# Squares of the SSD outputs get two tiles of their own instead of the tiles shared with the tanh of the silus

## The chip, the cores and the metric

The kernel runs on one core of one Trainium2 chip. The metric is the device time of one execution in microseconds (us). The kernel before takes 1710.79 us, the median of three runs (1707.15 to 1713.31).

## The reference

One layer of a hybrid recurrent decoder. A prompt of 2048 tokens and 8 samples of 8 tokens each (2112 rows of 1024 channels) are normalised and multiplied with one wide matrix (`w_in`). Three branches work on the product: a Mamba-2 style SSD scan, an RG-LRU and an S5. Their outputs, 2048 channels, are multiplied with `w_out`, added to the input and normalised again. Of the SSD branch this matters:

```
xbc = silu(causal_conv(xbc))                # 16 channel blocks of 128: x (8), B (4), C (4)
y   = ssd_scan(x, dt, a, B, C) + d * x      # chunks of 128 tokens, a state handed from chunk to chunk
y   = y * silu(z)
y_ssd = rmsnorm(y) * ssd_norm_g             # the mean of y*y over all 1024 SSD channels of a token
```

The mean needs the squares of all SSD outputs, summed over the channel blocks. The kernel adds them up, block by block, in tiles `sqacc`.

## The kernel before, in words

Channels lie on the 128 partitions, tokens on the free axis. The tokens are cut in five segments (`SEGS`): s = 0 to 3 are 512 prompt tokens each, s = 4 the 64 sample tokens. The input projection of one channel block and one segment is `in_proj` (L235): 24 matmuls of 512 columns, L247 to L249, into one bank of PSUM out of a ring of three (`pmm`). float32 is carried in two float16 halves, hence three matmuls per step.

The phases follow one another: projections and S5 inputs, S5, RG-LRU with the GLU, then the SSD branch, which fills about 697 to 1362 us of the profile, and last the output projection (L1175 to L1177). In the SSD branch `ssd_group` (L624) is called for four groups g = 0 to 3. For each segment (the sample segment goes with s = 2) it does three things.

- `channels` (L631), four times: two blocks of x, one of B, one of C. `in_proj`; ScalarE copies the bank to `raw` (L340, three buffers); the convolution is one ScalarE instruction (L353) and three on VectorE (L355); then silu: ScalarE writes a tanh into a tile `th` (L641) and VectorE forms `(th + 1) * x` (L642).
- `ssd_chunk` (L556), four times: transposes (L545, L546), scores (L520), the decay `e` (L524, L525 on ScalarE, L531 on VectorE), outputs into `ps_y` (L568, L571), the state (L573, L577, L578), and the outputs back into the x tiles (L582).
- `gated` (L645), twice, for the two x blocks: a gate `pz`, the product `x * pz` (L655 on VectorE), its store and its square `sq` on ScalarE (`Row.add`, L380 to L387; the square is L384), and on GpSimd the addition `sqacc += sq` (L662). For groups 0 and 1 `pz` was computed earlier and is loaded by a DMA (L650). For groups 2 and 3 it is computed here by `gate` (L357): an `in_proj`, a tanh into a tile `th` (L362 on ScalarE) and `pz = (th + 1) * ps` on VectorE (L363), which also sets the PSUM bank free.

The pool `st` has two buffers per tag. In the kernel before the tag `th` serves the tanh of `channels`, the tanh of `gate` and the squares `sq`; the tag `pz` is separate and has two buffers as well. For the first x block of group 0 the square goes straight into `sqacc`.

The order of each engine's queue is not written out by hand. A planner goes through the program with a simulated time line and places on each engine the earliest instruction of the program that is ready in its simulation, so that work of later segments can be drawn forward where an engine would idle. A tile that has no free buffer holds its writer back in that plan, too. The engines then run their queues in the planned order. Pools of different phases share memory (`sx` on the left side takes the place of the GLU's pool), and a tile waits for those tiles before it that lay at its addresses.

Of the kernel before, what the change touches and what calls it, by code (L numbers as in the profile page):

```python
# [8 lines left out]
F32 = mybir.dt.float32  # L9
# [15 lines left out]
SG = 512  # L25
SEGS = [(0, SG), (SG, SG), (2 * SG, SG), (3 * SG, SG), (SEQ, NS)]
# [16 lines left out]
def hymba_step_kernel(  # L43
# [11 lines left out]
    st = ctx.enter_context(tc.tile_pool(name="st", bufs=2))  # L55
# [28 lines left out]
    def col(nm, i, src=cols):  # L84
        c = COL[nm] + i
        return src[:, c:c + 1]
# [141 lines left out]
    def w_ahead(n=1):  # L228

        for c0 in W_ORDER[len(WB):len(WB) + n]:  # L230
            WB[c0] = Block(c0)
# [3 lines left out]
    def in_proj(w, s):  # L235

        n = SEGS[s][1]
        blocks = list(WB.values())
        for i, b in enumerate(blocks):
            if b.done is None and blocks[i - 6].left:  # L240
                b.age += 1
                if b.age > AGE:
                    b.finish()
            b.left = b.left or (b.w is w and s == 3)
        ps = bank(pmm, "mm", "ps_mm")
        for k in range(KD):
            P.matmul(ps[:, :n], lhsT=w[:, 0, k, :], rhs=XH[s][:, k, :], start=(k == 0), stop=False)  # L247
            P.matmul(ps[:, :n], lhsT=w[:, 0, k, :], rhs=XL[s][:, k, :], start=False, stop=False)  # L248
            P.matmul(ps[:, :n], lhsT=w[:, 1, k, :], rhs=XH[s][:, k, :], start=False, stop=(k == KD - 1))  # L249
        return ps[:, :n]  # L250

    def seg_tile(tag, name, s, pool, w=SG, bufs=None, wsmp=NS):
        if s == 4:
            return pool.tile([128, wsmp], F32, name=name + "s", tag=tag + "s", bufs=2 if pool is st else 1)
        return pool.tile([128, w], F32, name=name, tag=tag, bufs=bufs)
# [71 lines left out]
    def conv_raw(ps, un, s, tl, stT):  # L327

        raw = seg_tile("raw", "raw", s, st, SG + 3, 3, 88)
        if s == 4:  # L330
            rv = raw.rearrange("p (b e) -> p b e", e=11)
            G.tensor_copy(rv[:, :, 0:3], stT.rearrange("p (b e) -> p b e", e=3))
            A.activation(out=rv[:, :, 3:11], in_=ps.rearrange("p (b e) -> p b e", e=8), func=AF.Copy, scale=un)
            G.tensor_copy(tl.t27[:, 1:9, :], rv[:, :, 8:11])
            return raw
        if s == 0:
            G.memset(raw[:, 0:3], 0.0)
        else:
            G.tensor_copy(raw[:, 0:3], tl.halo)
        A.activation(out=raw[:, 3:SG + 3], in_=ps, func=AF.Copy, scale=un)  # L340
        tl.halo = tl.t27[:, 0, :] if s == 3 else tmp.tile([128, 3], F32, name="halo", tag="halo", bufs=6)
        G.tensor_copy(tl.halo, raw[:, SG:SG + 3])
        return raw

    def conv(out, raw, s, w, b):
        if s == 4:
            o = out.rearrange("p (b e) -> p b e", e=8)
            rv = raw.rearrange("p (b e) -> p b e", e=11)
            tap = [rv[:, :, j:j + 8] for j in range(4)]
        else:  # L350
            o = out
            tap = [raw[:, j:j + SG] for j in range(4)]
        A.activation(out=o, in_=tap[0], func=AF.Identity, scale=w[0], bias=b)  # L353
        for j in range(1, 4):
            V.scalar_tensor_tensor(o, tap[j], w[j], o, op0=ALU.mult, op1=ALU.add)  # L355

    def gate(ps, un2, s):  # L357

        n = SEGS[s][1]
        th = seg_tile("th", "th", s, st)  # L360
        pz = seg_tile("pz", "pz", s, st)
        A.activation(out=th, in_=ps, func=AF.Tanh, scale=un2)  # L362
        V.scalar_tensor_tensor(pz, th, 1.0, ps, op0=ALU.add, op1=ALU.mult)  # L363
        return pz
# [191 lines left out]
    def ssd_chunk(sp, g, xs, BT, CT, c, H):  # L556
        q0 = (c * 128) % SG
        bcq = sp.tile([128, 4, 128], F32, name="bcq", tag="bcq")
        S.dma_start(out=bcq, in_=aT[c, 4 * g:4 * g + 4, :].unsqueeze(0).to_broadcast([128, 4, 128]))
        xdt, xw, bs = transposed(sp, xs, BT, q0, 128, g, c)  # L560
        m = scores(sp, g, BT, CT, q0, 128, bcq, c)
        yp = bank(pss, "y", "ps_y")
        if c:
            ce = c_decayed(sp, CT, q0, 128, eT[c, 4 * g:4 * g + 4, :])
        o = [yp[64 * (h % 2):64 * (h % 2) + 64, (h // 2) * 128:(h // 2) * 128 + 128] for h in range(4)]
        for j in range(2):
            for h in (2 * j, 2 * j + 1):
                P.matmul(o[h], lhsT=xdt[:, h, :], rhs=m[:, h, :], start=True, stop=(c == 0))  # L568
            if c:
                for h in (2 * j, 2 * j + 1):  # L570
                    P.matmul(o[h], lhsT=H[:, h, :], rhs=ce[:, h, :], start=False, stop=True)  # L571
        ps = bank(pss, "s", "ps_s")
        P.matmul(ps[:, 0:256], lhsT=bs, rhs=xw.rearrange("p h e -> p (h e)"), start=True, stop=True)  # L573
        hn = sp.tile([128, 4, 64], F32, name="hst", tag="hst")
        spv = ps[:, 0:256].rearrange("p (h e) -> p h e", h=4)
        if c:
            G.tensor_tensor(hn, H, dec[:, c, 4 * g:4 * g + 4].unsqueeze(2).to_broadcast([128, 4, 64]), op=ALU.mult)  # L577
            V.tensor_tensor(hn, hn, spv, op=ALU.add)  # L578
        else:
            V.tensor_copy(hn, spv)  # L580
        for j in range(2):
            V.scalar_tensor_tensor(xs[j][:, q0:q0 + 128], xs[j][:, q0:q0 + 128], dpair[:, 2 * g + j:2 * g + j + 1],  # L582
                                   yp[:, j * 128:(j + 1) * 128], op0=ALU.mult, op1=ALU.add)
        return hn
# [39 lines left out]
    def ssd_group(sx, sp, g, done):  # L624
        blks = [2 * g, 2 * g + 1, 8 + g, 12 + g]
        ws = [WB[c0] for c0 in SB(g)]
        rows = [Row(k, unz[:, k:k + 1] if k < ZE else WB[k]) for k in (2 * g, 2 * g + 1)]
        tls = [Tail(b) for b in blks]
        H = None

        def channels(i, s):  # L631

            w, un, _ = ws[i]
            b = blks[i]
            raw = conv_raw(in_proj(w, s), un, s, tls[i], stS[:, b, :])
            if s == 3:
                w_ahead()
            x = seg_tile("xxbc"[i] + str(i % 2), "x", s, sx if i < 2 else sp, SG, 5 if i < 2 else 2)
            conv(x, raw, s, [col("sconv_w", 16 * j + b, hcols) for j in range(4)], col("sconv_b", b, hcols))
            th = seg_tile("th", "th", s, st)  # L640
            A.activation(out=th, in_=x, func=AF.Tanh)  # L641
            V.scalar_tensor_tensor(x, th, 1.0, x, op0=ALU.add, op1=ALU.mult)  # L642
            return x

        def gated(j, s, y):  # L645
            k = 2 * g + j
            s0, n = SEGS[s]
            if k < ZE:
                pz = seg_tile("pz", "pz", s, st)
                S.dma_start(out=pz, in_=zb[k, :, s0:s0 + n])  # L650
            else:
                pz = gate(in_proj(WB[k][0], s), WB[k][2], s)
                if s == 3:
                    w_ahead()
            V.tensor_tensor(y, y, pz, op=ALU.mult)  # L655
            if g == 0 and j == 0:
                sqacc[s] = sx.tile([128, SEGS[s][1]], F32, name="sqacc", tag=f"sqacc{s}", bufs=1)
                rows[j].add(s, y, sqacc[s])
            else:
                sq = seg_tile("th", "sq", s, st)  # L660
                rows[j].add(s, y, sq)
                G.tensor_tensor(sqacc[s], sqacc[s], sq, op=ALU.add)  # L662

        for segs in SSD_ORD:
            xb = {s: [] for s in segs}
            for i in range(4):
                for s in segs:
                    xb[s].append(channels(i, s))
            for s in segs:
                x0, x1, BT, CT = xb[s]  # L670
                if s == 4:
                    ssd_sample(sp, g, (x0, x1), BT, CT)
                else:
                    for c in range(4 * s, 4 * s + 4):
                        H = ssd_chunk(sp, g, (x0, x1), BT, CT, c, H)
            if 3 in segs:
                S.dma_start(out=o_ssd_p[g], in_=H)
                done()
            for j in range(2):
                for s in segs:  # L680
                    gated(j, s, xb[s][j])
# [608 lines left out]
    sx = pool(sA, "ssx", "left")  # L1290
# [8 lines left out]
    for i, (t0, n) in enumerate(TT_):  # L1299
        s = min(t0 // SG, 4)  # L1300
# [143 lines left out]
```

## Time and profile before

| | |
|---|---|
| time, median of three | 1710.79 us |
| the profiled execution's own time | 1712.97 us |
| its span in the profile | 1711.3 us |
| TensorE (PE) busy | 1594.9 us, 93% |
| VectorE (DVE) busy | 1108.0 us, 65% |
| ScalarE (ACT) busy | 861.3 us, 50% |
| GpSimd (POOL) busy | 534.0 us, 31% |

The profile is of one execution. A page gives busy times per engine and the groups of instructions that cost most; further views give busy times in chosen stretches, the instructions of one engine in order of time, who waited for whom, and the chain of work that ended last. A number in brackets behind an instruction is the time its engine sat idle ahead of it, with the instruction that ended this. PEclk is the clock that TensorE was granted, as a share of full speed.

### The profile page before, as it was taken

The numbers are of one execution on the slowest core, as the hardware profiler recorded it, in microseconds if no ns is written. First come the engines' busy times: TensorE is split into PE (matmuls) and PEld (weight loads), VectorE is DVE, ScalarE is ACT, GpSimd is POOL, SyncE is SP. The second block draws the span as 40 slices with busy tenths as digits, with TensorE's granted clock in tenths as the row PEclk, the third lists the DMA queues.
The fourth block names the chain that finished last, engine by engine and source line by source line (L and its number), as shares of the span: only waits on it lengthen the run. The fifth ranks groups of instructions, "written<-read, shape, count | busy, mean of one in ns | idle before, by whom it ended". The sixth has DMA issues, their size and how long they took to land.

```text
span 1711.3 us, 26615 instructions
## 1 busy us (share of the span) xinstructions
PE 1594.9 (93%) x9474; PEld 823.3 (48%) x9474; DVE 1108.0 (65%) x2643; ACT 861.3 (50%) x1913; POOL 534.0 (31%) x822
## 2 busy tenths in 40 slices
PE   6899898898899999999999968999999699999998
PEld 3554544454444444455555544555555444444443
DVE  7844578996676575678778566677777734633332
ACT  7723424443787776657466455566765421422210
POOL 1213226764131111344545555544454200000000
PEclk9999899999989999999999989999999699999999
DMA  7412322232325242333324253243325521633100
GB/s 241 127 46 53 113 93 89 90 101 68 99 85 156 80 138 66 105 86 122 117 91 131 86 153 81 69 142 115 115 93 191 175 80 63 207 99 99 43 25 31
DMA packets 143941, 178.17 MB, mean 104 GB/s; under 512 B 66424, under 2 KB 92480, under 8 KB 143808
## 3 DMA queue, kind: packets, MB, share of 16 engines
q1 hardware_dynamic: 143808, 176.47, 33.9%
q8 instruction: 74, 1.21, 0.3%
q14 instruction: 59, 0.48, 0.1%
HBM read 126.57 MB, written 48.69 MB: 102 GB/s over the span
## 4 chain that ended last, share of the span: by engine, by line
PE 47%; DVE 5%; ACT 4%; DMA 2%; issue 2%; POOL 2%; SPq 0%; POOLq 0%; ACTq 0%; DVEq 0%
PE ps_o L1175 7%; PE ps_o L1177 7%; PE ps_o L1176 6%; PE ps_mm L247 6%; PE ps_mm L248 6%; PE ps_mm L249 6%; PE ps_y L568 2%; DVE x L355 2%; PE ps_s L573 2%; PE ps_y L571 1%; DMA ce<-eT 1%; PE ps_g L520 1%; PE ps_tp L545 1%; DMA w<-in_w_blk_dram 1%; PE ps_o L1205 1%
## 5 line engine op out<-in xcount | busy, mean ns | idle before, releaser
L247 PE MATMUL ps_mm<-xh,whl 128*128 128x512 f16 x1280 | 494.0, 386 | 18.1 <-DVE pz L363 12.8
L248 PE MATMUL ps_mm<-xl,whl 128*128 128x512 f16 x1280 | 493.5, 386 | 0.0
L249 PE MATMUL ps_mm<-xh,whl 128*128 128x512 f16 x1280 | 492.6, 385 | 0.9 <-DVE whl L206 0.9
L248 PEld LDWEIGHTS <-whl 128*128 128x128 f16 x1600 | 155.9, 99 | 168.5 <-issue 38.3
L247 PEld LDWEIGHTS <-whl 128*128 128x128 f16 x1600 | 159.6, 101 | 149.1 <-issue 17.8
L249 PEld LDWEIGHTS <-whl 128*128 128x128 f16 x1600 | 156.4, 99 | 153.5 <-issue 18.1
L1175 PE MATMUL ps_o<-wo,yt 128*128 128x512 f16 x512 | 195.6, 382 | 10.2 <-ACT yt L1186 5.2
L1176 PE MATMUL ps_o<-wo,yt 128*128 128x512 f16 x512 | 195.6, 382 | 0.0
L1177 PE MATMUL ps_o<-wo,yt 128*128 128x512 f16 x512 | 194.7, 381 | 0.0
L355 DVE SCALAR_TENSOR_TENSOR x<-raw,hcols,x 128x512 f32<-128x512 f32 x192 | 158.5, 830 | 23.3 <-ACT x L353 20.6
L524 ACT ACTIVATE e<-bcq,acum 128x128 f32<-128x128 f32 (+1 forms) x272 | 86.1, 386 | 58.9 <-PE ps_y L568 52.5
L1186 ACT ACTIVATE yt<-y,rsc 128x256 f16<-128x256 f32 (+1 forms) x144 | 56.7, 477 | 106.0 <-PE ps_o L1177 81.0
L538 POOL TENSOR_TENSOR ce<-ce,x 128x512 f32<-128x512 f32 x60 | 84.8, 1422 | 66.8 <-DMA ce<-eT 31.8
L1347 ACT ACTIVATE yo<-res 128x1024 f32<-128x1024 f32 x16 | 16.8, 1050 | 153.4 <-DVE res L1195 153.4
L1195 DVE SCALAR_TENSOR_TENSOR res<-ps_o,rsu,res 128x512 f32<-128x512 f32 x32 | 24.0, 750 | 94.9 <-PE ps_o L1177 94.9
L1175 PEld LDWEIGHTS <-yt 128*128 128x128 f16 x512 | 50.5, 99 | 66.3 <-ACT yt L1186 5.6
L1176 PEld LDWEIGHTS <-yt 128*128 128x128 f16 x512 | 50.4, 98 | 66.3 <-issue 6.9
L363 DVE SCALAR_TENSOR_TENSOR pz<-th,ps_mm 128x512 f32<-128x512 f32 x64 | 43.6, 682 | 57.8 <-ACT th L362 57.3
L531 DVE TENSOR_TENSOR e<-e,gm 128x512 f32<-128x512 f32 (+1 forms) x68 | 57.2, 842 | 36.8 <-POOL gm L530 32.9
L1177 PEld LDWEIGHTS <-yt 128*128 128x128 f16 x512 | 50.3, 98 | 61.3 <-issue 0.8
L340 ACT ACTIVATE raw<-ps_mm,sc_out 128x512 f32<-128x512 f32 x80 | 54.2, 677 | 39.8 <-PE ps_mm L249 37.6
L362 ACT ACTIVATE th<-ps_mm,sc_out 128x512 f32<-128x512 f32 x64 | 43.6, 681 | 52.1 <-PE ps_mm L249 51.5
(450 smaller groups left out, 3012.8 us busy)
## 6 DMA issues: line engine op xcount, KB each, us to landing
w<-in_w_blk_dram SPq DMA_DIRECT2D x40, 512.0 KB
bcq<-aT SPq DMA_DIRECT2D x64, 256.0 KB
y<-ysp SPq DMA_DIRECT2D x16, 1024.0 KB
ce<-eT SPq DMA_DIRECT2D x60, 256.0 KB
xt<-in_x_dram SPq DMA_DIRECT2D x16, 512.0 KB
ysp<-x SPq DMA_DIRECT2D x32, 256.0 KB
wo<-in_w_out_dram SPq DMA_DIRECT2D x16, 512.0 KB
res<-in_x_dram SPq DMA_DIRECT2D x16, 512.0 KB
```

Source lines behind the costliest of these rows:

```text
L247: P.matmul(ps[:, :n], lhsT=w[:, 0, k, :], rhs=XH[s][:, k, :], start=(k == 0), stop=False)
L248: P.matmul(ps[:, :n], lhsT=w[:, 0, k, :], rhs=XL[s][:, k, :], start=False, stop=False)
L249: P.matmul(ps[:, :n], lhsT=w[:, 1, k, :], rhs=XH[s][:, k, :], start=False, stop=(k == KD - 1))
L340: A.activation(out=raw[:, 3:SG + 3], in_=ps, func=AF.Copy, scale=un)
L355: V.scalar_tensor_tensor(o, tap[j], w[j], o, op0=ALU.mult, op1=ALU.add)
L524: A.activation(out=e[:n, h, :n], in_=bcq[:n, h, :n], func=AF.Relu, scale=-1.0, bias=acum[:n, c, 4 * g + h:4 * g + h + 1])
L531: V.tensor_tensor(e[:n, :, :n], e[:n, :, :n], gm.unsqueeze(1).to_broadcast([n, 4, n]), op=ALU.mult)
L538: G.tensor_tensor(ce[:, :, :n], ce[:, :, :n], CT[:, q0:q0 + n].unsqueeze(1).to_broadcast([128, 4, n]), op=ALU.mult)
L1175: P.matmul(ps, lhsT=h, rhs=w[:, 0, c], start=(k == 0), stop=False)
L1176: P.matmul(ps, lhsT=h, rhs=w[:, 1, c], start=False, stop=False)
L1177: P.matmul(ps, lhsT=l, rhs=w[:, 0, c], start=False, stop=(k == nk - 1))
L1186: A.activation(out=hl[:, k, 0, :n], in_=r[:, k, :n], func=AF.Copy, scale=c)
```

## The change

The square of an SSD output no longer takes a tile of the tag `th`. It gets a tag `sq` of its own with two buffers of 128 x 512 float32 in the pool `sx` (4 KB more per partition). For the sample segment a part of the wide tile is used, where before there was a narrow one (`ths`). No instruction is added or taken away.

```
-                sq = seg_tile("th", "sq", s, st)
+                sq = sx.tile([128, SG], F32, name="sq", tag="sq", bufs=2)[:, :SEGS[s][1]]
                 rows[j].add(s, y, sq)
                 G.tensor_tensor(sqacc[s], sqacc[s], sq, op=ALU.add)
```

## Rows read from the trace of the kernel before

**Rows 1.** Busy time in stretches: us; busy (instructions) per engine; PEclk; DMA share; GB/s
```profile
697.00:985.00 288.00, 284.70 (x1922) 156.92 (x1919) 212.81 (x407) 168.82 (x395) 139.91 (x220) 1.00 0.37 108
985.00:1054.00 69.00, 49.36 (x325) 28.58 (x324) 41.47 (x87) 35.72 (x93) 36.18 (x47) 0.83 0.46 124
1054.00:1330.00 276.00, 268.33 (x1915) 149.74 (x1910) 204.89 (x435) 169.65 (x393) 131.06 (x187) 0.99 0.38 119
1330.00:1362.00 32.00, 19.09 (x83) 12.39 (x82) 24.21 (x55) 16.41 (x35) 7.63 (x8) 0.57 0.41 134
1362.00:1711.30 349.30, 339.37 (x1628) 155.24 (x1626) 141.61 (x331) 75.39 (x183) 2.87 (x3) 0.99 0.26 86
```
**Rows 2.** TensorE in order of time: start, us, instruction, [idle before <- releaser]
```profile
987.30 0.44 PE L545 MATMUL ps_tp<-id,x 128*128 128x128 f32 x2 [2.14 <-DVE x L642]
996.24 0.38 PE L249 MATMUL ps_mm<-xh,whl 128*128 128x512 f16 x1
1021.86 1.53 PE L545 MATMUL ps_tp<-id,x 128*128 128x128 f32 x4 [7.48 <-DVE x L642]
1036.45 0.44 PE L568 MATMUL ps_y<-e,xdt 128*64 128x128 f32 x4 [0.89 <-DVE e L531]
1040.08 0.44 PE L571 MATMUL ps_y<-ce,hst 128*64 128x128 f32 x4 [1.30 <-POOL ce L538]
1044.78 0.58 PE L247 MATMUL ps_mm<-xh,whl 128*128 128x512 f16 x1 [3.82 <-DVE pz L363]
1254.61 0.38 PE L247 MATMUL ps_mm<-xh,whl 128*128 128x512 f16 x1 [0.71 <-ACT raw L340]
1355.61 0.59 PE L1175 MATMUL ps_o<-wo,yt 128*128 128x512 f16 x1 [2.71 <-DVE y_m L115]
```
**Rows 3.** ScalarE in order of time, squares and tanhs
```profile
1018.46 0.71 ACT L384 ACTIVATE sq<-x,unz 128x512 f32<-128x512 f32 x1
1019.93 0.63 ACT L641 ACTIVATE th<-x 128x512 f32<-128x512 f32 x1 [0.67 <-POOL sqacc L662]
1023.27 0.69 ACT L362 ACTIVATE th<-ps_mm,sc_out 128x512 f32<-128x512 f32 x1
1042.63 0.71 ACT L384 ACTIVATE sq<-x,sc_out 128x512 f32<-128x512 f32 x1
1043.34 0.66 ACT L362 ACTIVATE th<-ps_mm,sc_out 128x512 f32<-128x512 f32 x1
```
**Rows 4.** VectorE in order of time: products, gates and the silu's second step
```profile
1015.55 0.69 DVE L655 TENSOR_TENSOR x<-x,pz 128x512 f32<-128x512 f32 x1
1016.48 0.69 DVE L655 TENSOR_TENSOR x<-x,pz 128x512 f32<-128x512 f32 x1
1024.61 0.68 DVE L363 SCALAR_TENSOR_TENSOR pz<-th,ps_mm 128x512 f32<-128x512 f32 x1
1174.36 1.69 DVE L642 SCALAR_TENSOR_TENSOR x<-th,x 128x512 f32<-128x512 f32 x1
1354.88 0.67 DVE L363 SCALAR_TENSOR_TENSOR pz<-th,ps_mm 128x512 f32<-128x512 f32 x1
```
**Rows 5.** TensorE, instructions of L247 alone (eight to one in_proj), in stretches
```profile
946.00:983.00 37.00, 15.56 (x41) 4.01 (x41) 1.00 0.31 90
1017.00:1026.00 9.00, 0.00 (x0) 0.00 (x0) 0.50 0.56 136
```
**Rows 6.** ScalarE, instructions of L340 alone (one to a channel block), same stretch
```profile
946.00:983.00 37.00, 2.05 (x3) 1.00 0.31 90
```
**Rows 7.** The chain that ended last, in order of time: start, us, what
```profile
1045.36 0.43 PE ps_mm L248
1051.01 0.21 PE ps_mm L247
```
**Rows 8.** Costliest waits, 700 to 1365 us: total us, times, longest
```profile
ACT th L641 <- POOL sqacc L662: 10.3, 11, 1.4
```
**Rows 9.** GpSimd in order of time, the addition of a square
```profile
1173.82 1.68 POOL L662 TENSOR_TENSOR sqacc<-sqacc,sq 128x512 f32<-128x512 f32 x1 [1.53 <-ACT sq L384]
```

## The prediction, made before the result was known

> **What bounds the kernel now.** I read the busy times by stretch first, then TensorE's own idle times in the stretch that stands out, then the queues of ScalarE and VectorE around them. By stretch, TensorE is the bound: in the SSD phase it works 284.7 of 288 us from 697 to 985, and 268.3 of 276 from 1054 to 1330; behind it, in the output projection, 339.4 of 349.3 [rows 1]. Nothing that lies beside it pays there. Two stretches are different: 985 to 1054, with 19.6 us idle and a granted clock of 0.83, and 1330 to 1362, with 12.9 us idle at 0.57 [rows 1]. The idle time of the first is mostly in three waits: 2.14, 7.48 and 3.82 us [rows 2].
>
> Two of them end with the silu's VectorE step (L642), the third with a gate (L363). Both need a `th` tile. The ScalarE rows show how these come: a tanh of `channels` at 1019.93 waits for the GpSimd addition of a square, the gate's tanh at 1023.27 comes behind it, and the next gate's tanh at 1043.34 directly behind the next square at 1042.63 [rows 3]. The reader is to see more than the 10.3 us in 11 waits that the list of waits names [rows 8]. The tiles of a tag go out in program order, and in that order the tanhs of segment s + 1 stand behind the squares of segment s. A square exists only when the SSD outputs of its segment are done. So no silu and no gate of a later segment can be computed before an earlier segment's last chunk is through, though its projection and convolution were drawn forward long before.
>
> That also stops TensorE's filler. From 946 to 983 us, 41 L247 are 5 projections, of which ScalarE took only 3 as `raw` [rows 5, 6]; the other two were gates of group 2, and one more projection ran until 996.5 [rows 2]. Three gates fill the ring of three PSUM banks, and each keeps its bank until its L363. From then to 1026 no projection runs (none of L247 in 1017 to 1026 [rows 5]); one runs when the first gate ends at 1024.61 + 0.68 us [rows 4]; the next starts at 1044.78, when the second gate lets go [rows 2].
>
> **The change, part by part.** No instruction is added or taken away; the 4 KB cost no time. The additions on GpSimd stay. What changes is which waits exist, and with them the planned order from the first square on.
>
> The tanh of a channel block then waits for tiles of other tanhs alone. The gates get a new limit: `pz` has two tiles too, so a gate's L363 waits for the product L655 two places before it. In the stretch at hand these end at 1016.24 and 1017.17 [rows 4], so two gates can be finished about 1017 to 1018 and give back two banks, instead of at 1025.3 and 1044.7.
>
> (a) The wait of 7.48 us (1014.4 to 1021.9) ends when the first bank is free, about 1017.2: 4.7 us saved. Between 1.4 (the two gaps that the additions leave in front of the tanhs, about 0.7 each [rows 3]) and 7.5.
>
> (b) 0.89, 1.30 and 3.82 us idle between 1035 and 1044.8 [rows 2]: with free banks the projections of the next gate and of the next channel blocks are there to fill them, some 5 us each. 6.0 saved; at least 0 if the plan places them elsewhere, at most 6.2.
>
> (c) 2.14 us at 987.3: the x tile was convolved long before and waited for its tanh alone. 2.1 saved, between 0 and 2.1.
>
> (d) The clock. Behind the 3.82 us the projection's matmuls take 0.43 us each, the lower of the two levels, and 0.21 from 1051 at the latest [rows 7]: up to half of 6.2 us, 3.1. The four L545 behind the 7.48 us take 1.53 us [rows 2], half of it or more the same loss. I take 3.5, between 0 and 4.4.
>
> (e) The end of the phase. The last gate's L363 runs at 1354.88 [rows 4], and TensorE waits for a bank until 1355.61, 2.71 us [rows 2]. With the gate done 30 us earlier that goes, but the low halves of `yt` come only behind the same work on VectorE. I take 0.7, between 0 and 2.7.
>
> (f) 0.71 us at 1254.61, a `raw` behind squares and a gate's tanh [rows 2]: 0.7, between 0 and 0.7.
>
> Sum: 4.7 + 6.0 + 2.1 + 3.5 + 0.7 + 0.7 = 17.7 us. Against it I set 3 us: a TensorE that is ahead meets other limits sooner (the B and C tiles have two buffers, the weights are converted just ahead of use), so that some of the 7.7 us idle in the 276 us behind the gap [rows 1] will grow; its size is a choice. Net 14.7. The profiled execution took 1712.97 us, 2.2 above the median of 1710.79; from it 1698.3, from the median 1696.
>
> What would be late next: the chunk's own chain and the loads of the decay rows, to which I put the rest of the 19.6 us, some 4 us (19.6 less 2.14, 7.48, 0.89, 1.30 and 3.82), where the gates wait for L655 of the old segment even in the new kernel. I leave these in place.
>
> A rule that speaks against the change. At 1174.36 an L642 takes 1.69 us, while the addition on GpSimd, from 1173.82, takes 1.68 [rows 4, 9]; a product of the same size takes 0.69 [rows 4]. The Trainium skill, SBUF — State Buffer, section SBUF: two separate sides, says that a VectorE operation with two SBUF inputs and a GpSimd operation that reads SBUF lock each other out for a whole instruction. The pair of rows agrees. Today the tanh waits for the addition in 11 places, which keeps its L642 apart from it; without that wait more of them may meet. By that rule the slower rival below gets 1 us more per boundary.
>
> **The rivals.** *Nothing measurable.* TensorE's idle time is moved, not filled: the run-ahead stops at `pz` or at the B and C tiles, and the waits come back as waits for the chunk chain, or the filler used earlier is missing at the end, where 12.9 us are idle already. For it: a chunk needs the state of the one before it, and no filler shortens that. Against it: 276 us with 7.7 idle follow, so TensorE remains the bound behind the gap. Only (c), a part of (a) and the gaps at the additions remain: about 3 us, 1708.
>
> *Slower.* The tanhs and L642 are drawn forward into VectorE's and ScalarE's in-order queues and there stand ahead of the chunk chain (L531, L582, L578). Place: the last chunks of a segment; price: four L642 of 0.69 us, 2.8 us per boundary between segments, of which there are 15. It decides when more than 6 boundaries show it on TensorE (17.7 / 2.8). At 9 it is 25 - 17 = 8 us slower, 1719. For it: the order is planned on simulated times, and today's plan already makes TensorE wait for L531 [rows 2]. Against it: TensorE has filler at nearly all boundaries. By the skill's rule above it would be 3.8 us per boundary and 1727 at 9; I put 0.04 of this rival's chance there.
>
> *More.* The new plan also fills the 4 us left over above and takes the whole of (a), (d) and (e), and something of the 12.9 us at the end: 28 us, 1683.
>
> That the change doesn't do what it says would need the square's tile to wait by its two buffers: pairs of squares lie some 24 us apart (1018 and 1042 [rows 3]) and an addition takes under 2 us [rows 9], so both tiles are free by then. I leave it at nothing.
>
> **How the numbers follow.** The forecast has 0.55 (its own range 1686 to 1705), nothing measurable 0.20, slower 0.17, more 0.08. About 0.3%, 5 us, is what a measurement of this kernel can tell from no change. Faster by more: nearly all of 0.55, a third of 0.20, all of 0.08: 0.66. Within: most of 0.20, the edges of the others: 0.19. Slower: 0.15. The upper bounds of (a) to (f) together give 23.6 us, and with the 4 us and some of the end 30: 1681 is the low end. The high end goes into the slower case: 1716.
>
> **What would show it.** Right: no tanh L641 waits for L662; the tanhs stand apart from the squares; the gates' tanhs in groups 2 and 3 run well ahead of the squares, bounded by L655; the time without any L247 behind about 996 us ends near 1017 and doesn't come again before 1045; from 985 to 1054 TensorE idles 9 us or less; ahead of the first square nothing differs. Wrong: the gates still follow the squares; or TensorE's waits for L531, L582 and L578 grow by more than 10 us in the phase; or the idle time at the end grows by what is saved before.

## The result and the profile after

The changed kernel takes 1682.38 us, the median of six runs (1680.86 to 1683.68); the kernel before took 1710.6 us beside it (1706.6 to 1716.1). The ratio is 0.9824 (95%: 0.9804 to 0.9844), 28 us less. Forecast were 1696 us and a gain of 14.7: the sign is right, the size is about half of what came. The time is that of the rival called *more*.

The profiled execution took 1682.5 us, its span is 1680.8. Busy time by stretch, as in [rows 1] (us; busy and instructions of PE, PEld, DVE, ACT, POOL; PEclk; DMA share; GB/s), of the changed kernel:

```profile
697.00:985.00 288.00, 280.30 (x1948) 157.42 (x1947) 232.40 (x426) 176.55 (x425) 155.86 (x233) 1.00 0.40 121
985.00:1054.00 69.00, 69.00 (x497) 38.62 (x496) 52.34 (x105) 42.41 (x111) 41.43 (x58) 1.00 0.37 106
1054.00:1330.00 276.00, 262.19 (x1786) 148.72 (x1784) 204.60 (x459) 167.55 (x375) 128.94 (x172) 0.95 0.41 127
1330.00:1362.00 32.00, 32.00 (x149) 14.39 (x147) 17.80 (x43) 12.93 (x32) 0.00 (x0) 0.99 0.54 162
1362.00:1680.80 318.80, 308.88 (x1480) 140.76 (x1478) 122.65 (x280) 63.67 (x155) 0.00 (x0) 0.99 0.23 77
```

From 985 to 1054 us TensorE has no idle time at all, where it had 19.6 us, and the clock there is 1.00 instead of 0.83. The end of the SSD phase, with its low clock, now lies inside the third row: the output projection begins at 1325.59 us, 25 us earlier than before (its first matmul stood at 1351.01; the one in [rows 2], at 1355.61, comes behind a second wait). The span is 30.5 us shorter. Sorted by stretch (idle is the length less PE's busy time, in us):

| | idle before | idle after | saved | forecast |
|---|---|---|---|---|
| 0 to 697 | 62.99 | 62.16 | 0.8 | 0 |
| 697 to 985 | 3.30 | 7.70 | -4.4 | 0 |
| 985 to 1054 | 19.64 | 0 | 19.6 | 12.8 (a, b, c) |
| 1054 to 1362 | 20.58 | 13.81 | 6.8 | 1.4 (e, f), less the 3 |
| after 1362 | 9.93 | 9.92 | 0 | 0 |
| PE busy, same 9474 matmuls (clock) | 1594.86 | 1587.22 | 7.6 | 3.5 (d) |
| sum | | | 30.5 | 14.7 |

Now the same rows that the prediction worked from. ScalarE of the changed kernel in order of time, at the boundary that [rows 3] show (squares L384, gates' tanhs L362, channels' tanhs L641):

```profile
974.51 0.69 ACT L362 ACTIVATE th<-ps_mm,sc_out 128x512 f32<-128x512 f32 x1 [2.52 <-PE ps_mm L249]
980.34 0.69 ACT L362 ACTIVATE th<-ps_mm,sc_out 128x512 f32<-128x512 f32 x1 [0.81 <-PE ps_mm L249]
996.06 0.71 ACT L384 ACTIVATE sq<-x,unz 128x512 f32<-128x512 f32 x1
...
996.79 0.72 ACT L384 ACTIVATE sq<-x,unz 128x512 f32<-128x512 f32 x1
...
998.08 0.62 ACT L641 ACTIVATE th<-x 128x512 f32<-128x512 f32 x1
1005.91 0.63 ACT L641 ACTIVATE th<-x 128x512 f32<-128x512 f32 x1 [4.50 <-DVE x L355]
```

The first two gates' tanhs stand 22 and 16 us ahead of these squares; before, both came behind them. The squares themselves are 22 us earlier than in [rows 3]. VectorE at the same place, which answers to [rows 4]:

```profile
995.05 0.68 DVE L655 TENSOR_TENSOR x<-x,pz 128x512 f32<-128x512 f32 x1
995.98 0.77 DVE L655 TENSOR_TENSOR x<-x,pz 128x512 f32<-128x512 f32 x1
996.68 0.67 DVE L363 SCALAR_TENSOR_TENSOR pz<-th,ps_mm 128x512 f32<-128x512 f32 x1
997.88 0.67 DVE L363 SCALAR_TENSOR_TENSOR pz<-th,ps_mm 128x512 f32<-128x512 f32 x1
```

The limit that the prediction named is there: both L363 come directly behind L655, so two PSUM banks are held, from about 974 and 980 us until 997 and 998. But TensorE doesn't stop for it. L247 alone, in the stretches behind those of [rows 5] (us; PE and PEld busy; PEclk; DMA share; GB/s):

```profile
983.00:1017.00 34.00, 12.46 (x33) 3.14 (x32) 1.00 0.35 105
1017.00:1026.00 9.00, 3.88 (x11) 1.08 (x11) 1.00 0.35 119
```

Before, the same stretches have 10 and 0 instructions of L247. The list of waits from 700 to 1365 us (total us, times, longest), against [rows 8]; no L641 waits for L662 any more:

```profile
ACT th L641 <- DVE x L355: 99.5, 46, 4.5
```

That sum was 21.3 us in 10 waits before. The tanh of a channel now waits for its own convolution, one by one; before, four came in a row when the squares were done. Where this starts is seen at the first squares of all. The kernel before, squares and channels' tanhs on ScalarE:

```profile
742.85 0.71 ACT L384 ACTIVATE sqacc<-x,unz 128x512 f32<-128x512 f32 x1
...
744.41 0.71 ACT L384 ACTIVATE sq<-x,unz 128x512 f32<-128x512 f32 x1
...
745.11 0.61 ACT L641 ACTIVATE th<-x 128x512 f32<-128x512 f32 x1
...
747.15 1.14 ACT L641 ACTIVATE th<-x 128x512 f32<-128x512 f32 x2
...
748.96 0.63 ACT L641 ACTIVATE th<-x 128x512 f32<-128x512 f32 x1
...
779.20 0.72 ACT L384 ACTIVATE sqacc<-x,unz 128x512 f32<-128x512 f32 x1 [0.47 <-DVE x L655]
```

and the changed kernel:

```profile
719.08 0.63 ACT L641 ACTIVATE th<-x 128x512 f32<-128x512 f32 x1 [3.36 <-DVE x L355]
...
724.57 0.63 ACT L641 ACTIVATE th<-x 128x512 f32<-128x512 f32 x1 [1.39 <-DVE x L355]
...
730.89 0.63 ACT L641 ACTIVATE th<-x 128x512 f32<-128x512 f32 x1 [0.28 <-DVE x L355]
...
737.19 0.63 ACT L641 ACTIVATE th<-x 128x512 f32<-128x512 f32 x1 [0.97 <-DVE x L355]
...
742.76 0.72 ACT L384 ACTIVATE sqacc<-x,unz 128x512 f32<-128x512 f32 x1
...
766.44 0.72 ACT L384 ACTIVATE sqacc<-x,unz 128x512 f32<-128x512 f32 x1 [0.85 <-DVE x L655]
```

The four tanhs of segment 1 are through at 737.8 instead of 749.6 us, ahead of the squares of segment 0, and the chunks of segment 1 end 13 us earlier: the next square comes at 766.4 instead of 779.2. TensorE shows nothing of it, it is busy in both kernels. What differs is what it is busy with. The chunks' last VectorE step, L582 (two to a chunk), counted in stretches, before:

```profile
697.00:900.00 203.00, 10.76 (x36) 1.00 0.36 106
900.00:985.00 85.00, 5.95 (x20) 1.00 0.39 113
985.00:1054.00 69.00, 4.80 (x16) 0.83 0.46 124
697.00:1054.00 357.00, 21.51 (x72) 0.97 0.39 111
```

and after:

```profile
697.00:900.00 203.00, 13.09 (x44) 1.00 0.40 119
900.00:985.00 85.00, 4.44 (x16) 1.00 0.40 126
985.00:1054.00 69.00, 6.26 (x22) 1.00 0.37 106
697.00:1054.00 357.00, 23.79 (x80) 1.00 0.40 118
```

An instruction that runs across a border is counted on both sides of it, so the rows add up to 2 more than the whole stretch has after the change. By 900 us the changed kernel is 8 L582, four chunks, ahead; the lead is 4 at 985 us (60 against 56) and 8 again at 1054. The kernel before had done more projections instead: 37 L340 from 697 to 985 us, against 34. Then it has little left to fill the time: from 985 to 1054 it does 2 more L340 and 16 L582, the changed kernel 7 and some 20.

### The profile page after: what moved, and what is told of

Same layout as the page of the kernel before. It is cut to its first block, busy times and chain, and to the rows that moved or that the text cites. A ratio compares the mean times of both kernels' runs of the same rounds, so it can differ in the third digit from the quotient of the medians.

```text
span 1680.8 us, 26643 instructions
## 1 busy us (share of the span) xinstructions
PE 1587.2 (94%) x9474; PEld 820.9 (49%) x9474; DVE 1112.0 (66%) x2643; ACT 858.2 (51%) x1913; POOL 540.9 (32%) x822
## 4 chain that ended last, share of the span: by engine, by line
PE 44%; DVE 7%; DMA 3%; ACT 3%; issue 2%; POOL 2%; SPq 0%; POOLq 0%; ACTq 0%; DVEq 0%
PE ps_o L1175 7%; PE ps_o L1176 7%; PE ps_o L1177 7%; PE ps_mm L248 5%; PE ps_mm L247 5%; PE ps_mm L249 5%; DVE x L355 3%; PE ps_y L568 1%; PE ps_s L573 1%; PE ps_y L571 1%; DMA ce<-eT 1%; PE ps_s L618 1%; DMA wo<-in_w_out_dram 1%; DVE e L531 1%; PE ps_tp L545 1%
## 5 line engine op out<-in xcount | busy, mean ns | idle before, releaser
L247 PE MATMUL ps_mm<-xh,whl 128*128 128x512 f16 x1280 | 492.0, 384 | 11.1 <-DVE pz L363 7.3
L247 PEld LDWEIGHTS <-whl 128*128 128x128 f16 x1600 | 159.0, 101 | 145.3 <-issue 15.2
L355 DVE SCALAR_TENSOR_TENSOR x<-raw,hcols,x 128x512 f32<-128x512 f32 x192 | 173.6, 904 | 38.1 <-ACT x L353 35.9
L1186 ACT ACTIVATE yt<-y,rsc 128x256 f16<-128x256 f32 (+1 forms) x144 | 56.7, 477 | 109.9 <-PE ps_o L1177 81.1
L641 ACT ACTIVATE th<-x 128x512 f32<-128x512 f32 x64 | 40.1, 627 | 100.9 <-DVE x L355 100.6
L363 DVE SCALAR_TENSOR_TENSOR pz<-th,ps_mm 128x512 f32<-128x512 f32 x64 | 43.6, 682 | 55.2 <-ACT th L362 54.7
L531 DVE TENSOR_TENSOR e<-e,gm 128x512 f32<-128x512 f32 (+1 forms) x68 | 57.2, 841 | 28.5 <-POOL gm L530 23.8
L362 ACT ACTIVATE th<-ps_mm,sc_out 128x512 f32<-128x512 f32 x64 | 43.7, 682 | 61.9 <-PE ps_mm L249 61.3
```

Of the source, the lines that this page charges most:

```text
L531: V.tensor_tensor(e[:n, :, :n], e[:n, :, :n], gm.unsqueeze(1).to_broadcast([n, 4, n]), op=ALU.mult)
L1186: A.activation(out=hl[:, k, 0, :n], in_=r[:, k, :n], func=AF.Copy, scale=c)
```

## The experiments

Theory 1: tiles of a shared tag, handed out in program order, put every tanh of the next segment behind the squares of this one, so the chunks start late, and TensorE fills the time with projections that it later lacks. Theory 2: only the waits of the tanhs for GpSimd's additions cost. Theory 3: any other plan would do. Theory 4: it is where tiles lie in memory. Each time stands beside the kernel before on the same chip.

**Two unused tiles.**

```
                 sq = seg_tile("th", "sq", s, st)
+                sx.tile([128, SG], F32, name="pad", tag="pad", bufs=2)
```

> The kernel before with two further 128x512 float tiles taken from the same pool at the line of the change and never written: same memory as the changed kernel, same order of work as before. Theory 1 (the shared tiles put every tanh of the next segment behind the squares of the segment before, so the order in which chunks and projections interleave changes), theory 2 (only the wait of single tanhs for GpSimd's additions costs) and theory 3 (any other plan would do) all expect no change, 1708 to 1713 us. Theory 4 (where tiles lie in memory matters) expects part of the gain, under 1703.

1713.62 against 1714.33 us, ratio 1.0 (0.9984 to 1.0015): no gain. Theory 4 falls.

**No addition of the squares.**

```
-                G.tensor_tensor(sqacc[s], sqacc[s], sq, op=ALU.add)
```

> The kernel before without GpSimd's addition of the squares (L662), so the squares of all blocks but the first are left out of the row sums; the tiles stay shared and a square still holds a tile, but is freed as soon as ScalarE has written it. Theory 2 (the 10.3 us in which tanhs wait for the additions) expects most of the 28 us, 1682 to 1692. Theory 1 (a tanh of the next segment stays behind the square itself, which is behind the chunks) expects little, 1700 to 1710.

1708.1 against 1714.33, ratio 0.9956 (0.9937 to 0.9974). The order is another one too (theory 3), and 18.5 us of idle stay between 985 and 1054. Theories 2 and 3 together explain 6 of the 28 us (11 at the end of the interval), and that includes what GpSimd gains by doing less work.

**Own tiles, old order.** `SQS` holds the last two squares.

```
-            A.activation(out=th, in_=x, func=AF.Tanh)
+            with behind(*SQS): A.activation(out=th, in_=x, func=AF.Tanh)
```

and the same for the gate's tanh at L362, on top of the change.

> The changed kernel, squares in tiles of their own, but every tanh of a channel and of a gate is put behind the last two squares issued before it on ScalarE, as the shared tiles did, with no wait for GpSimd's additions. Theory 1 (the order) expects most of the gain gone, 1700 to 1715. Theory 2 (the waits for the additions alone) expects it kept, 1682 to 1690.

1728.68 against 1714.33, ratio 1.0071 (1.0047 to 1.0096): the whole gain is gone, and more than theory 1 expected. ScalarE in order of time:

```profile
741.77 0.71 ACT L384 ACTIVATE sq<-x,unz 128x512 f32<-128x512 f32 x1
742.47 1.14 ACT L641 ACTIVATE th<-x 128x512 f32<-128x512 f32 x2
744.96 0.63 ACT L641 ACTIVATE th<-x 128x512 f32<-128x512 f32 x1 [1.35 <-DVE x L642]
746.07 0.62 ACT L641 ACTIVATE th<-x 128x512 f32<-128x512 f32 x1
```

The tanhs stand behind the squares in one cluster as in the kernel before, and no L641 waits for L662 here. So the place in the order is enough for the loss, without the wait. Why it is 14 us slower than the kernel before stays open; this rule holds every tanh behind both squares, which the two shared tiles need not do for each.

**Four tiles, still mixed.** A second ring `tb` of two tiles takes gate 1, square 1 and the tanhs of channels 2 and 3:

```
+            th = sx.tile([128, SG], F32, name="th", tag="tb", bufs=2)[:, :SEGS[s][1]] if i > 1 else seg_tile("th", "th", s, st)
```

> The same four tiles as in the changed kernel, in two rings of two that each still mix squares with tanhs: gate 0, square 0 and channels 0 and 1 in one, gate 1, square 1 and channels 2 and 3 in the other. Theory 1 (what counts is that tanhs are queued behind squares) expects little of the gain, 1700 to 1712, unless a ring twice as long lets the gates of the next segment go ahead. A theory by which the number of tiles counts expects most of it, 1682 to 1690.

1708.15 against 1714.33, ratio 0.9953 (0.9938 to 0.9968). As many tiles as in the changed kernel give about a quarter of its gain; which work shares them is what counts.

**Gates' tanhs alone in own tiles**, and **channels' tanhs alone in own tiles**, squares left where they were:

```
+                pz = gate(in_proj(WB[k][0], s), WB[k][2], s, sx.tile([128, SG], F32, name="tg", tag="tg", bufs=2)[:, :SEGS[s][1]])
```

```
-            th = seg_tile("th", "th", s, st)
+            th = sx.tile([128, SG], F32, name="tc", tag="tc", bufs=2)[:, :SEGS[s][1]]
```

> Squares and the channels' tanhs still share two tiles; the gates' tanhs get two tiles of their own (the same memory as the change). If the gates (their PSUM banks, the 7.48 us wait at 1021.86) carry the gain, 1685 to 1698; if the silus of the channels, and through them the chunks, carry it, 1702 to 1713. The sum on which the prediction rests put 10.7 of its 17.7 us on the gates (the 4.7 us of the bank, and the 6.0 us of idle behind it), so it expects 1692 to 1700 here.

> The other half alone: the channels' tanhs get two tiles of their own, squares and gates' tanhs still share two. If the channels' silus carry the gain, 1683 to 1693; if the gates carry it, 1702 to 1713. The prediction's sum has 2.1 to 3 us that belong to channels alone, so by it 1705 to 1710.

Gates: 1701.15 against 1714.66, ratio 0.9916 (0.9899 to 0.9933), 13.5 us; that lies just outside both ranges that were expected. Channels: 1686.73, ratio 0.9836 (0.9804 to 0.9869), 27.9 us, all of the gain within the interval. The stretch 985 to 1054 us with the gates' tiles:

```profile
985.00:1054.00 69.00, 58.08 (x419) 33.74 (x420) 48.97 (x98) 37.29 (x100) 36.57 (x51) 0.90 0.44 123
```

and with the channels', in an execution of 1682.9 us, the fastest of its four:

```profile
985.00:1054.00 69.00, 68.00 (x492) 38.44 (x493) 52.06 (x103) 42.79 (x108) 40.25 (x56) 1.00 0.36 100
```

Freeing the gates takes 8.7 of the 19.6 us there; freeing the channels takes 18.6, with the gates still behind the squares. The two gains together are more than the 28 us of the change, so in part they fill the same idle time.

**By groups.** Own tiles for the squares in some groups only (`if g < 2 else` the shared tile, and so on):

> Squares have tiles of their own in groups 0 and 1 only, shared ones in groups 2 and 3. Until 697 us the gates come from memory, so little is projected beside the chunks there. If the gain comes from the stretch 985 to 1054 us and what is behind it, as the idle shows, 1704 to 1711. If the plan of the first half already decides (the new plan runs less far ahead with its projections from the start), 1690 to 1703.

> Squares have tiles of their own in groups 2 and 3 only. If the gain belongs to the second half, 1682 to 1692; if part of it is made in the first half, 1692 to 1705.

> Squares have tiles of their own in group 0 alone. In the trace of the changed kernel the second pair of squares comes at 766.4 us instead of 779.2, so chunks are 13 us early at the second boundary already. If the lead is made once and kept, 1685 to 1693 (as with groups 0 and 1: 1689). If every boundary adds its share, and groups 0 and 1 hold 8 of 16, a quarter to a half of 25 us, 1700 to 1708. If it is lost again in group 1, 1705 to 1713.

> Squares have tiles of their own in group 1 alone. If each group adds its own share, 26 less 8 is 18 us: 1693 to 1700 with the kernel before at 1713 to 1715. If group 1's gain needs the lead from group 0, 1704 to 1712. If group 1 alone decides, since its squares stand ahead of the silus that end at 985 to 1020 us, 1686 to 1692.

| own tiles in groups | time | before | ratio (95%) |
|---|---|---|---|
| 0 and 1 | 1689.06 | 1714.66 | 0.9839 (0.9817 to 0.9860) |
| 2 and 3 | 1700.93 | 1714.66 | 0.9911 (0.9894 to 0.9928) |
| 0 | 1706.25 | 1714.91 | 0.9959 (0.9942 to 0.9976) |
| 1 | 1699.70 | 1714.72 | 0.9915 (0.9892 to 0.9938) |

Groups 0 and 1, where no gate is computed, hold 26 of the 28 us, and the first expectation, which went by where the idle is seen, is refuted. Group 0 is the clean case: its last squares stand at 872.69 and 873.42 us, in a stretch where TensorE idled 3.3 us (697 to 985), and it gives 9 us (4 to 10 by the interval of the ratio). Group 1 is not so clean: its last squares (1018.46 in [rows 3]) are those that stand ahead of the wait of 7.48 us, so part of its 15 us is idle time that the prediction saw. With own tiles there, the idle time from 985 to 1054 us is 3.6 instead of 19.6 us, and from 697 to 985 it is 11.4 instead of 3.3. Both groups together give 26, about the sum of 9 and 15; single boundaries were not tried. Groups 2 and 3 would give 14 by themselves; on top of 0 and 1 they add 3 to 7 us, and the intervals of the two ratios overlap.

Where group 0's 9 us are gained stays open. Its time lies in two of the three ranges that were expected and doesn't decide between them. Its profile is of an execution of 1712.98 us, 6.7 above the median of the eight; in it the lead of four L582 at 900 us (40 against 36) is gone at 985 (56 in both).

**Holding the projections back**, in the kernel before; `LAST` holds the matmul L573 of each segment's last chunk:

```
-            raw = conv_raw(in_proj(w, s), un, s, tls[i], stS[:, b, :])
+            with behind(*[LAST[4 * g + (s, 2)[s == 4] - 2]] if g or s > 1 else []): raw = conv_raw(in_proj(w, s), un, s, tls[i], stS[:, b, :])
```

> The kernel before, squares in the shared tiles; the projections of a segment's channels are held behind the last chunk of the segment two before it, so they can't run more than two segments ahead (at 985 us it was 2.75). If running ahead was itself the harm (projections taking TensorE from chunks that were ready), 1685 to 1700. If the chunks are late because their silus are behind the squares, the projections only fill the time, and holding them back moves the idle time forward: 1708 to 1725.

1712.94 against 1714.91, ratio 0.9988 (0.9974 to 1.0003): no change in the time, though this is another plan too (theory 3). Its busy times by stretch:

```profile
697.00:985.00 288.00, 268.04 (x1857) 152.46 (x1856) 217.97 (x414) 171.62 (x413) 151.93 (x223) 0.98 0.41 113
985.00:1054.00 69.00, 66.16 (x396) 35.02 (x395) 39.59 (x78) 32.48 (x79) 26.64 (x40) 0.98 0.34 98
```

The gap of 985 to 1054 is gone (2.8 us), and 20.0 us idle stand from 697 to 985, where there were 3.3: 22.8 us together, against 22.9 before. L582 up to 1054 us: 72, as before; in the changed kernel 80. So the gap at 985 was no fault of that place. It is what the chunks owe by then, and running ahead with projections only decided when it showed.

**Smaller and other tiles.** One tile for squares; one tile for squares and a third gate tile; squares written into the gate's tile (`sq = pz`), which is dead after L655, so that no memory is added; the same with two more gate tiles:

> The changed kernel with one tile for the squares instead of two (2 KB). What has counted so far is that the channels' tanhs are no longer behind squares; a square would now wait for the addition of the square before it, up to 1.7 us, with little behind it in ScalarE's queue. Theory 1: 1682 to 1692, nearly the whole gain. Theory that two free tiles for squares are needed: 1695 to 1710.

> One tile for the squares, and the 2 KB saved go to a third gate tile: the second block's gate pz has a one-tile ring of its own. The prediction held that gates, and with them PSUM's banks, are freed only behind L655 of the segment before (4 us of the idle left in place). If that limit still costs, this is 3 to 8 us faster than the kernel with one square tile; if the interleaving has removed it, within 3 us of it.

> No extra memory: a square is written into the gate's tile pz, which is dead after the product L655, so the tanhs keep two tiles of the tag th to themselves. Channels' and gates' tanhs are free of squares, as in the changed kernel, but pz is freed later (after square and addition, some 3 to 4 us). Theory 1: 1683 to 1695, most of the gain with no memory. If the gates' tiles are the tight ones, 1695 to 1712.

> Squares in the gate's tile, and the 4 KB that the change spends on squares go to two more gate tiles (two per block). If gate tiles limit, this is the fastest of all, 1670 to 1680; if the interleaving alone counts, it is within 3 us of the changed kernel, 1680 to 1686.

| | time (before: 1713.05) | ratio (95%) |
|---|---|---|
| one square tile | 1684.44 | 0.9841 (0.9811 to 0.9871) |
| one, and a third gate tile | 1683.32 | 0.9827 (0.9808 to 0.9847) |
| squares in the gate's tile | 1679.84 | 0.9802 (0.9784 to 0.9819) |
| the same, four gate tiles | 1682.72 | 0.9825 (0.9810 to 0.9840) |

All lie within 5 us. More gate tiles gain nothing that can be measured: the limit seen at 996 us costs nothing once the silus are free. The third one, with no memory added, looked some 2 us faster than the changed kernel, so the two ran side by side:

> The changed kernel once more, for the comparison with the next one on the same chip: 1680 to 1685.

> Squares written into the gate's tile, no memory more than before: 1677 to 1682, that is 1 to 4 us faster than the changed kernel if the first run of it was no chance; within 1 us of it otherwise.

1679.93 and 1680.16 us against 1714.91, both with ratio 0.9799 (0.9778 to 0.9820). It is no faster; it does the same without the 4 KB.

## Why the prediction was right in sign and half in size

*The cause* was named rightly: tiles of a tag go out in program order, and the tanhs of the next segment stand behind the squares. The old order alone, put back over the new tiles, takes the whole gain away, and leaving out the additions on GpSimd gains only 6 us.

*The step that failed* is the one before the sum: "By stretch, TensorE is the bound: in the SSD phase it works 284.7 of 288 us from 697 to 985 [...]. Nothing that lies beside it pays there." Own tiles in group 0 alone, whose squares all lie in that stretch and for which the sum has no term, pay 9 us (4 to 10); in groups 0 and 1 they pay 26, where the sum has only the waits of 2.14 and 7.48 us behind group 1's squares. TensorE was busy with work taken forward, while the chunks fell behind (36 L582 by 900 us against 44). The sum was read only from idle time that TensorE showed, mostly in one stretch, and there from the waits for gates.

*(a) and (b)*, 10.7 us, were the gates' part. Gates freed alone gain 13.5 us: not far off by themselves. But the silus got only (c), 2.1 us, for one wait of 2.14 us, and the silus freed alone gain 27.9. This is the term that was mis-sized most. The 7.48 us of (a) end with a silu (L642) too; the prediction priced them by the gate's bank, and with the silus alone freed TensorE idles 1.0 us from 985 to 1054.

*The 4 us left in place*, "where the gates wait for L655 of the old segment even in the new kernel": the gates do wait there (L363 at 996.68 behind L655 at 995.98), and the idle time went all the same, since TensorE then had the projections of channels that the old plan had used up. All 19.6 us came, not 12.8.

*(d)*, 3.5 us with 0 to 4.4 as its bounds: PE's busy time for the same matmuls fell by 7.6 us. The dip of 0.83 from 985 to 1054 is gone; the one at the end of the phase, 0.57, came along. A second profiled execution of the changed kernel has 1582.7 us of PE where the first has 1587.2, so executions of one kernel differ by 4.5 us in this term. The bound was too narrow: it counted only the matmuls directly behind two waits.

*(e), (f)*: 1.4 us forecast, 6.8 came between 1054 and 1362. Of it 3.8 us are from 1054 to 1295, where the idle fell from 7.3 to 3.5 us, and 3.0 from the end of the phase, where it was 13.3 us (1295 to 1362) and is 10.3 (1295 to 1330). The bank's wait of (e), 2.71 us, is gone. Ahead of the first matmul of the output projection TensorE waits for the ScalarE copy `yt` (L1186), before and after:

```profile
1351.01 0.61 PE L1175 MATMUL ps_o<-wo,yt 128*128 128x512 f16 x1 [5.24 <-ACT yt L1186]
1325.59 0.61 PE L1175 MATMUL ps_o<-wo,yt 128*128 128x512 f16 x1 [2.96 <-ACT yt L1186]
```

The two waits together fell by 5.0 us, of which other waits took 2 back. The sum did not have the first of them, and the chunks arrive with a lead: the phase's last squares are at 1318.2 instead of 1361.5 us.

*The 3 us against it* were right in kind and wrong in place: the idle grew by 4.4 us ahead of 985, where chunks are now what TensorE waits for, and not behind 1054.

*Of the signs*: no L641 waits for L662, the first gates are ahead of the squares and bounded by L655, projections run from 983 to 1026, and 0 us idle from 985 to 1054 meet the "9 us or less". "Ahead of the first square nothing differs" was wrong, and it was the sign that mattered: the tanhs at 719 to 737 us lie ahead of the first square of 742.8. They could be there because squares no longer come before them in the ring. Of the signs of being wrong none came: TensorE's waits for L531, L582 and L578 fell from 9.6 to 6.0 us in the phase.

*The rivals.* *Slower* did not come: L642 drawn forward did not stand in the chunks' way. By the Trainium skill's rule in SBUF — State Buffer, section SBUF: two separate sides, which the rows of before bore out in one place, more L642 might have met the additions on GpSimd. The L642 themselves took less: the 64 of 512 columns from 697 to 1365 us had a mean of 862 ns before, and after 814 (busy us, mean ns | idle before):

```profile
L642 DVE SCALAR_TENSOR_TENSOR x<-th,x 128x512 f32<-128x512 f32 x64 | 52.1, 814 | 14.0 <-ACT th L641 13.7
```

Other VectorE operations with two inputs in SBUF took longer, though: the 32 products L655 went from 698 to 774 ns, and the 192 steps of the convolution, before and after, from 830 to 904:

```profile
L355 DVE SCALAR_TENSOR_TENSOR x<-raw,hcols,x 128x512 f32<-128x512 f32 x192 | 158.5, 830 | 23.3 <-ACT x L353 20.6
L355 DVE SCALAR_TENSOR_TENSOR x<-raw,hcols,x 128x512 f32<-128x512 f32 x192 | 173.6, 904 | 38.1 <-ACT x L353 35.9
```

These two take 17 us more, of which other operations gave most back: VectorE's busy time went from 1108.0 to 1112.0 us. That they met GpSimd more often is not shown, and the kernel got faster all the same.

*Nothing measurable*, where idle is only moved, is what holding the projections back did: 22.8 us idle against 22.9. It doesn't describe the change, since the change starts the chunks earlier. *More*, at 0.08, was the right size by parts of the right reasons: it had the rest of the 19.6 us, the clock and the end, but not the first half.

## What to carry to other kernels

A busy engine in a stretch only says that it had something to do. Where a planner may draw work forward, ask which work fills it: count the steps of the chain that can't be drawn forward (here L582) against the filler (L340) at a few times, and size a change by what it gives that chain, not by the idle time at the place where the filler ran out. And before giving a tile a ring of its own, look which users of the shared ring are made late by another's data; where a dead tile can take the late user, the same gain costs no memory.

## What the runs showed of the hardware

Executions of one kernel differ by more than the 3.5 us that were forecast for the clock: the changed kernel's two profiled executions had a mean granted clock of 0.971 and 0.976, PE busy 1587.2 and 1582.7 us, spans of 1680.8 and 1677.3 us. Two profiled executions of the same order of work before (the kernel itself and the one with unused tiles) agreed at 0.965 and 1594.9 us.
